# A two-layer hybrid encoder on one core: three changes to the order of TensorE's work

## The chip, the cores and the metric

The program runs on one core of a Trainium2 chip. The metric is the device time of one execution in microseconds, the median of several runs; lower is better. Nothing is computed on the host but the repacking of the weights into chunks.

## The reference

The input is one sequence of 512 tokens with 1024 channels in float32. Each of the two layers is

```
hn = rmsnorm(x); proj = hn @ w_in
(aq, ak, av, bx, by, cq, ck, cv, dq, dk, dv, gl) = split(proj)
ya = dense attention with q/k norm and 2-D rotary      # mixer A, 8 heads on 2 key heads
yb = bidirectional linear recurrence with gates        # mixer B
yc = windowed attention with a sink logit              # mixer C
yd = three dilated window attentions, combined by their softmax denominators   # mixer D
gates = sigmoid(gl + gate_bias)                        # one per branch and channel
merged = sum over branches of gates * (y @ w_proj)
x = x + merged @ w_out
x = x + square(relu(rmsnorm(x) @ w_mlp1)) @ w_mlp2
```

and a last rmsnorm follows. In mixer D three groups of four heads are each normalised by themselves, and the output of a head is the sum of its three group outputs, weighted by a softmax over the groups' log denominators. Those weights are known only when all three groups are done.

## The kernel before

**Weights.** All weights come as chunks of 128x1024 float32 (512 KB) in the order of use. SP loads a chunk into one of three buffers (`raw`, L102), ScalarE (ACT) casts it to the short float32 format (`whi`, L118), and VectorE (DVE) takes the rest, raw minus high (`wlo`, L127). Three pairs of `whi` and `wlo` exist. A load into a `raw` buffer has to wait until cast and difference of the chunk three places earlier have read that buffer. Activations are split in the same way (`xh`, `xl`), and every product of 128 by 128 by 512 is three TensorE matmuls: high by high, high by low, low by high (`mm3`, L173 to L182).

**Which work goes beside which.** The heads of the attentions wait on DVE and ACT for their softmax, so their steps are mixed with steps of plain projections, here called fill. A fill step is a quarter of a gate chunk or half of a short projection: 6 matmuls. `merge` (L1100) mixes two generators a and b: it takes a step of a, then steps of b in the ratio nb to na. `MG` and `E1`, `E2`, `E3`, `FN` (L41, L43) are its tables: na, nb and the number of fill steps that go ahead of the even mixing.

**Attention A.** The loads of its keys and queries (`K`, `Q`) are issued, then the values of A and C are computed (`values_ac`, L527), then `merge` starts. The first step of a is the first head's first score (L796); three fill steps of branch B's gates follow.

**Attention C** is mixed with the values of D (`values_d`, L668): three groups, each with two weight chunks (u = 0, 1) for the contraction's first and second half, and four blocks of 128 tokens; each block is one `mm3` with 24 matmuls of 256 columns, cut into two steps.

**End of mixer D** (`attn_d_end`, L1041). It loads the denominators `W` of the three groups back from DRAM, lets `E1` yields pass, computes the weights on DVE and ACT (L1053 to L1065), transposes them on TensorE (`ps_misc`, L1069), copies the result (`wr`) and stores it to DRAM (`wd`), and then loads it eight times spread over 64 partitions (`wb`, `d_weight`, L1094): that is all three groups of the first half of the heads (hp = 0) and the first group of the second half. After `E2` yields it multiplies and adds the groups of the first half (L1086 to L1089) and splits the sum into `yD`, lets `E3` yields pass, and does the same with the second half; only there the last four `wb` loads are issued. The fill beside it is branch D's own: four gate chunks of 16 steps, and then the projection of `yD`, which is the first thing that needs both halves. The chunk of that projection is called PR below, the gate chunks GL0 to GL3, and the next ones GL4 and on.

All loads and stores named here stand on one queue, SP's, which issues in program order.

Of the kernel before, what the change touches and what calls it, by code (L numbers as in the profile page):

```python
# [37 lines left out]
    "h4 v5 n2 e1 l4 q8 s0 t3 o6 p7",  # L38
)]

MG = ((35, 48, 3), (41, 71, 2), (18, 47, 12))  # L41

E1, E2, E3, FN = (1, 5, 2, 15)  # L43

WU, P0, P1 = (16, 2, 2)

# [29 lines left out]
class Body:  # L76
# [96 lines left out]
    def mm3(self, ps, st, mv, n, step=0):  # L173
        mm = self.nc.tensor.matmul
        for k in range(n):
            (sh, sl), (mh, ml) = st(k), mv(k)
            mm(ps, sh, mh, start=(k == 0), stop=False)  # L177
            mm(ps, sh, ml, start=False, stop=False)  # L178
            mm(ps, sl, mh, start=False, stop=(k == n - 1))  # L179
            if step and k % step == step - 1 and k < n - 1:  # L180
                yield
        self.lows()  # L182

    def several(self, keys, mv, cuts):
# [483 lines left out]
    def values_d(self):  # L668

        nc = self.nc  # L670
        last = []
        for g in range(3):
            hls = self.take2("VD", g)
            for c in range(4):
                ps = self.ps("mm")
                yield from self.paced(last, self.mm3(
                    ps[:, 0:256],
                    lambda k: (self.xh[:, k, c * 128:(c + 1) * 128], self.xl[:, k, c * 128:(c + 1) * 128]),
                    lambda k: tuple(t[:, (k % 4) * 256:(k % 4 + 1) * 256] for t in hls[k // 4]), KD, 4))
                last.append(lambda ps=ps, g=g, c=c: self.value_d(ps, g, c))  # L680
                yield
        while last:
            last.pop()()
# [413 lines left out]
            r = 4 * g + 2 * hp + a  # L1097
            self.nc.sync.dma_start(out=t[64 * a:64 * (a + 1)], in_=wd[r:r + 1, :].to_broadcast([64, S]))

    def merge(self, a, b, na, nb, first=0):  # L1100

        e = 0
        live = [True, True]

        def step(i):
            if live[i] and next((a, b)[i], StopIteration) is StopIteration:
                live[i] = False

        step(0)
        for _ in range(first):  # L1110
            step(1)
        while any(live):
            step(0)
            e += nb - first
            while e >= na or not live[0]:
                step(1)
                e -= na
                if not any(live):
                    break


    def layer(self, l):
# [16 lines left out]
        with tc.tile_pool(name=f"aA{l}", bufs=1, reuse_waits="tile") as self.ap:  # L1139
            attn = self.attn_gqa(l, 0, yA)  # L1140
            next(attn)
            self.values_ac()
            self.merge(attn, self.fill(l, 1, self.yB), *MG[0])
        yC = self.y0p.tile([128, 2, 4, S], F32R, tag="y", name="yC")
        with tc.tile_pool(name=f"aC{l}", bufs=1, reuse_waits="tile") as self.ap:
            self.merge(self.attn_gqa(l, 2, yC), chain(self.values_d(), self.fill(l, 0, yA)), *MG[1])
        yD = y1p.tile([128, 2, 4, S], F32R, tag="y", name="yD")
        fill = self.fill(l, 3, yD)
        with tc.tile_pool(name=f"aD{l}", bufs=1, reuse_waits="tile") as self.ap:
            self.merge(self.attn_d(l, yD), self.fill(l, 2, yC), *MG[2])  # L1150
            self.merge(self.attn_d_end(yD), (next(fill) for _ in range(FN)), E1 + E2 + 1 + 2 * E3, FN)
# [330 lines left out]
```

## Time and profile before

| | |
|---|---|
| median of 3 runs | 2031.62 us (2030.08 to 2032.27) |
| profiled execution | 2030.6 us |
| its span, first to last instruction | 2028.8 us |
| TensorE (PE) busy | 2008.3 us, 99% |
| VectorE (DVE) busy | 1270.8 us, 63% |
| ScalarE (ACT) busy | 974.1 us, 48% |
| share of PE in the chain that ended last | 89% |
| mean granted TensorE clock | 0.996 of full speed |
| DMA, mean over the span | 112 GB/s |

TensorE is the engine to look at: it is busy nearly all the time, so the other engines matter only where TensorE waits for them. Matmul records overlap: a 512-column matmul lasts 0.39 us in its record, and the next one starts 0.228 us after it. So the distance between starts is what a matmul costs.

### The profile page before, as it was taken

How to read it: one execution, taken by the hardware profiler on the slowest of the kernel's cores; microseconds unless marked ns; L12 is line 12 of the kernel's file. 1: busy time of each engine (PE TensorE's matmuls, PEld its weight loads, DVE VectorE, ACT ScalarE, POOL GpSimd, SP SyncE). 2: the span in 40 equal slices, each digit the busy share in tenths (PEclk: the TensorE clock that was granted, in tenths of full speed). 3: DMA queues.
4: the chain of work that ended last, by engine and by line, in shares of the span. 5: the costliest groups of instructions: out<-in, count | busy, mean ns of one | idle time of the engine just before them, and what ended most of it. 6: DMA issues, size and time to landing. Idle time of an engine off the chain costs nothing.

```text
span 2028.8 us, 25698 instructions
## 1 busy us (share of the span) xinstructions
PE 2008.3 (99%) x9752; PEld 1665.0 (82%) x9752; DVE 1270.8 (63%) x2274; ACT 974.1 (48%) x1701; POOL 0.2 (0%) x4
## 2 busy tenths in 40 slices
PE   9999999999999999999999999999999999999998
PEld 7888789887778888888878888898877888888887
DVE  6889775764466544444658897758644665444445
ACT  4357786854534332322323668868445334322322
POOL 0000000000000000000000000000000000000000
PEclk9999999999999999999999999999999999999998
DMA  5454425332134233223335552152421522323231
GB/s 191 136 158 142 130 67 146 116 125 84 53 114 138 94 102 94 96 94 104 123 105 166 156 166 94 62 160 91 135 73 48 173 94 94 104 94 97 94 100 63
DMA packets 87439, 227.03 MB, mean 112 GB/s; under 512 B 15098, under 2 KB 21370, under 8 KB 87316
## 3 DMA queue, kind: packets, MB, share of 16 engines
q1 hardware_dynamic: 84436, 221.20, 34.5%
q10 hardware_dynamic: 2880, 4.20, 0.6%
q8 instruction: 77, 1.26, 0.3%
q14 instruction: 46, 0.38, 0.1%
HBM read 201.08 MB, written 24.27 MB: 111 GB/s over the span
## 4 chain that ended last, share of the span: by engine, by line
PE 89%; DVE 6%; ACT 2%; issue 1%; DMA 1%; SPq 0%; DVEq 0%; ACTq 0%
PE ps_mm L177 13%; PE ps_mm L178 13%; PE ps_mm L179 13%; PE ps_s L177 6%; PE ps_s L178 6%; PE ps_s L179 6%; PE ps_t L177 6%; PE ps_t L179 6%; PE ps_t L178 6%; PE ps_o L856 2%; PE ps_t L835 2%; PE ps_s L796 1%; PE ps_s L797 1%; DVE tt L338 1%; DVE wlo L127 1%
## 5 line engine op out<-in xcount | busy, mean ns | idle before, releaser
L118 ACT CAST whi<-raw 128x1024 fp32r<-128x1024 f32 (+1 forms) x318 | 329.0, 1041 | 334.9 <-PE ps_mm L178 105.6
L127 DVE TENSOR_TENSOR wlo<-raw,whi 128x1024 fp32r<-128x1024 f32 (+1 forms) x318 | 385.0, 1215 | 98.6 <-ACT whi L118 95.6
L177 PE MATMUL ps_mm<-xh,whi 128*128 128x512 f32 x720 | 289.0, 401 | 0.0
L179 PE MATMUL ps_mm<-xh,wlo 128*128 128x512 f32 x720 | 282.6, 392 | 0.0
L178 PE MATMUL ps_mm<-xl,whi 128*128 128x512 f32 x720 | 282.5, 392 | 0.0
L177 PEld LDWEIGHTS ps_mm<-xh,whi 128*128 128x128 f32 x720 | 136.1, 189 | 32.4 <-issue 4.1
L179 PEld LDWEIGHTS ps_mm<-xh,wlo 128*128 128x128 f32 x720 | 135.9, 189 | 29.8
L178 PEld LDWEIGHTS ps_mm<-xl,whi 128*128 128x128 f32 x720 | 136.2, 189 | 26.7
L177 PE MATMUL ps_t<-xh,whi 128*128 128x512 f32 x368 | 143.7, 390 | 0.0
L178 PE MATMUL ps_t<-xl,whi 128*128 128x512 f32 x368 | 143.3, 389 | 0.0
L179 PE MATMUL ps_t<-xh,wlo 128*128 128x512 f32 x368 | 143.2, 389 | 0.0
L177 PE MATMUL ps_s<-xh,whi 128*128 128x512 f32 x352 | 138.6, 394 | 0.0
L179 PE MATMUL ps_s<-xh,wlo 128*128 128x512 f32 x352 | 137.1, 390 | 0.0
L178 PE MATMUL ps_s<-xl,whi 128*128 128x512 f32 x352 | 137.0, 389 | 0.0
L845 DVE TENSOR_TENSOR PT<-ps_t,PT 128x512 fp32r<-128x512 f32 (+2 forms) x128 | 75.1, 587 | 63.9 <-ACT PT L842 54.7
L829 ACT ACTIVATE P<-P,al 128x512 f32<-128x512 f32 (+2 forms) x128 | 82.6, 645 | 17.0 <-DVE al L828 15.7
L719 DVE TENSOR_TENSOR gt<-ps_mm,rb 128x512 f32<-128x512 f32 x54 | 37.2, 688 | 78.3 <-PE ps_mm L179 77.9
L842 ACT CAST PT<-ps_t 128x512 fp32r<-128x512 f32 (+2 forms) x128 | 63.8, 500 | 46.6 <-PE ps_o L856 43.1
L177 PEld LDWEIGHTS ps_t<-xh,whi 128*128 128x128 f32 x368 | 69.1, 188 | 17.3 <-issue 3.0
L179 PEld LDWEIGHTS ps_t<-xh,wlo 128*128 128x128 f32 x368 | 69.1, 188 | 14.3
L178 PEld LDWEIGHTS ps_t<-xl,whi 128*128 128x128 f32 x368 | 69.1, 188 | 14.2
L177 PEld LDWEIGHTS ps_s<-xh,whi 128*128 128x128 f32 x352 | 66.1, 188 | 14.9 <-issue 1.4
(423 smaller groups left out, 4218.2 us busy)
## 6 DMA issues: line engine op xcount, KB each, us to landing
raw<-in_w_dram SPq DMA_DIRECT2D x314, 512.0 KB, 3.5
qsA<-stk SPq DMA_DIRECT2D x32, 128.0 KB, 2.3
qsC<-stk SPq DMA_DIRECT2D x32, 128.0 KB, 2.3
K<-ks SPq DMA_DIRECT2D x16, 256.0 KB, 6.0
Q<-qsA SPq DMA_DIRECT2D x16, 256.0 KB, 3.8
Q<-qsC SPq DMA_DIRECT2D x16, 256.0 KB, 7.0
qD<-stkf SPq DMA_DIRECT2D x24, 128.0 KB, 2.2
kD<-stkf SPq DMA_DIRECT2D x24, 128.0 KB, 2.2
```

The costliest lines, as they stand in the source:

```text
L118: self.nc.scalar.copy(hi[:, s], self.raws[i][:, s])
L127: self.nc.vector.tensor_tensor(out=lo[:, s], in0=raw[:, s], in1=hi[:, s].bitcast(F32), op=ALU.subtract)
L177: mm(ps, sh, mh, start=(k == 0), stop=False)
L178: mm(ps, sh, ml, start=False, stop=False)
L179: mm(ps, sl, mh, start=False, stop=(k == n - 1))
L338: nv.tensor_tensor(out=o, in0=a, in1=b, op=ALU.mult)
L719: nv.tensor_tensor(out=g, in0=ps, in1=self.rb, op=ALU.mult)
L829: ns.activation(out=P[:, 0:n], in_=P[:, 0:n], func=AF.Copy, scale=ls)
L835: nc.tensor.transpose(pt[:, b * 128:(b + 1) * 128], P[:, b * 128:(b + 1) * 128], self.ident)
L842: ns.copy(st["dst"][0], st["src"])
L845: nv.tensor_tensor(out=st["dst"][1], in0=st["src"], in1=st["dst"][0].bitcast(F32), op=ALU.subtract)
L856: nc.tensor.matmul(o, a, b, start=(n_ == 0), stop=(n_ == len(mm) - 1))
```

## The change

Three places change. First, ahead of attention A's first score four fill steps are issued (before: none), and one more behind it; `MG[0]` has a fourth number for that, and `merge` an argument. Second, `E1` goes from 1 to 3 and `FN` from 15 to 17: two more fill steps stand between the loads of `W` and the transposition of the weights, and the fill beside the end of mixer D is two steps longer. Third, the values of D use `mm3s` in place of `mm3`: the same 24 matmuls a block, but the eight that read the low part of the weights come last; the cut into two steps stays at 12 matmuls.

```diff
-MG = ((35, 48, 3), (41, 71, 2), (18, 47, 12))
-E1, E2, E3, FN = (1, 5, 2, 15)
+MG = ((35, 48, 5, 4), (41, 71, 2), (18, 47, 12))
+E1, E2, E3, FN = (3, 5, 2, 17)
...
+    def mm3s(self, ps, st, mv, n, step=0):
+
+        mm = self.nc.tensor.matmul
+        for k in range(n):
+            (sh, sl), mh = st(k), mv(k)[0]
+            mm(ps, sh, mh, start=(k == 0), stop=False)
+            mm(ps, sl, mh, start=False, stop=False)
+            if step and 4 * k == 3 * n - 4:
+                yield
+        for k in range(n):
+            mm(ps, st(k)[0], mv(k)[1], start=False, stop=(k == n - 1))
+        self.lows()
...
-                yield from self.paced(last, self.mm3(
+                yield from self.paced(last, self.mm3s(
...
-    def merge(self, a, b, na, nb, first=0):
+    def merge(self, a, b, na, nb, first=0, before=0):
...
-        step(0)
-        for _ in range(first):
-            step(1)
+        for i in range(first + 1):
+            if i == before:
+                step(0)
+            if i < first:
+                step(1)
```

**TensorE around the first score of attention A in the first layer.** `ps_t` belongs to the last block of values, `ps_mm` to a gate chunk. Before:

```order
L179 MATMUL ps_t_1947<-whi_1758,xl_84 128x256
L796 MATMUL ps_s_1976<-K_1852,Q_1855 128x512 [waits DMAHW2_49,DMAHW3_49,DMAHW1_49,DVE_49]
L797 MATMUL ps_s_1976<-K_1852,Q_1855 128x512
L177 MATMUL ps_mm_1985<-xh_83,whi_1792 128x512 [waits DVE_49,Activation_49]
L178 MATMUL ps_mm_1985<-xl_84,whi_1792 128x512
```

Now, where all 24 matmuls of the first gate chunk (weights `whi_1792`) stand ahead, and the first step of the second chunk (`whi_1974`, `wlo_1975`) comes right behind the score:

```order
L177 MATMUL ps_mm_1980<-xh_83,whi_1792 128x512
L178 MATMUL ps_mm_1980<-xl_84,whi_1792 128x512
L179 MATMUL ps_mm_1980<-xh_83,wlo_1793 128x512
L809 MATMUL ps_s_2010<-K_1852,Q_1855 128x512 [waits DMAHW3_49,DMAHW2_49,DMAHW1_49]
L810 MATMUL ps_s_2010<-K_1852,Q_1855 128x512
L177 MATMUL ps_mm_2020<-xh_83,whi_1974 128x512 [waits DVE_49,Activation_49]
L178 MATMUL ps_mm_2020<-xl_84,whi_1974 128x512
L179 MATMUL ps_mm_2020<-xh_83,wlo_1975 128x512 [waits DVE_49]
```

The score has moved behind a whole gate chunk, and the second gate chunk's weights are now wanted directly after it.

**SP's queue at the end of mixer D in the first layer.** `wb` are the spread weights, `raw` the weight chunks. Before:

```order
L1098 DMA wb_5631<-wd_4736 64x512
L102 DMA raw_5657<-in_w_dram 128x1024 [waits DMAHW2_49,DVE_49]
L102 DMA raw_5698<-in_w_dram 128x1024 [waits DMAHW3_49,DVE_49]
L1098 DMA wb_5716<-wd_4736 64x512 [waits DMAHW4_49,DVE_49]
L1098 DMA wb_5716<-wd_4736 64x512 [waits DMAHW5_49]
L1098 DMA wb_5720<-wd_4736 64x512 [waits DMAHW6_49,DVE_49]
L1098 DMA wb_5720<-wd_4736 64x512 [waits DMAHW7_49]
L102 DMA raw_5745<-in_w_dram 128x1024 [waits DMAHW0_49,DVE_49,Activation_49]
```

Now:

```order
L1111 DMA wb_5643<-wd_4736 64x512
L102 DMA raw_5657<-in_w_dram 128x1024 [waits DMAHW2_49,DVE_49,Activation_49]
L102 DMA raw_5691<-in_w_dram 128x1024 [waits DMAHW3_49,DVE_49]
L102 DMA raw_5732<-in_w_dram 128x1024 [waits DMAHW4_49,DVE_49,Activation_49]
L1111 DMA wb_5744<-wd_4736 64x512 [waits DMAHW5_49]
L1111 DMA wb_5744<-wd_4736 64x512 [waits DMAHW6_49]
L1111 DMA wb_5748<-wd_4736 64x512 [waits DMAHW7_49]
L1111 DMA wb_5748<-wd_4736 64x512 [waits DMAHW0_49]
```

The third `raw` load, which reuses the buffer of the PR chunk and so waits for that chunk's cast and difference, now stands ahead of the last four `wb` loads; before, it stood behind them.

**DVE at the same place.** The `og` rows multiply and add the groups of the second half of the heads; the `wlo` row without another wait is that of the PR chunk. Before:

```order
L719 TENSOR_TENSOR gt_5687<-ps_s_5659,rb_86 128x512 [waits PE_49]
L1086 TENSOR_TENSOR og_5301<-og_5301,wb_5631 128x512 [waits DMAHW1_49,DMAHW0_49]
L1086 TENSOR_TENSOR og_5474<-og_5474,wb_5716 128x512 [waits DMAHW5_49,DMAHW4_49]
L1086 TENSOR_TENSOR og_5575<-og_5575,wb_5720 128x512 [waits DMAHW7_49,DMAHW6_49]
L1088 TENSOR_TENSOR og_5301<-og_5301,og_5474 128x512 [waits DVE_49]
L1089 TENSOR_TENSOR og_5301<-og_5301,og_5575 128x512 [waits DVE_49]
L159 TENSOR_TENSOR yD_4728<-og_5301,yD_4728 128x512 [waits Activation_49]
L127 TENSOR_TENSOR wlo_5696<-raw_5605,whi_5695 128x1024
```

Now:

```order
L159 TENSOR_TENSOR yD_4728<-og_5118,yD_4728 128x512 [waits Activation_49]
L127 TENSOR_TENSOR wlo_5689<-raw_5585,whi_5688 128x1024 [waits DMAHW0_49]
L732 TENSOR_TENSOR gt_5728<-ps_t_5693,rb_86 128x512 [waits PE_49]
L1099 TENSOR_TENSOR og_5301<-og_5301,wb_5643 128x512 [waits DMAHW1_49,DMAHW0_49]
L1099 TENSOR_TENSOR og_5474<-og_5474,wb_5744 128x512 [waits DMAHW6_49,DMAHW5_49]
L1099 TENSOR_TENSOR og_5575<-og_5575,wb_5748 128x512 [waits DMAHW7_49,DMAHW0_49]
L1101 TENSOR_TENSOR og_5301<-og_5301,og_5474 128x512 [waits DVE_49]
L1102 TENSOR_TENSOR og_5301<-og_5301,og_5575 128x512 [waits DVE_49]
L159 TENSOR_TENSOR yD_4728<-og_5301,yD_4728 128x512 [waits Activation_49]
```

The PR chunk's difference has moved from behind the second half to between the first half (`og_5118`) and the second; the gates of GL1 (`gt_5687`) and GL2 (`gt_5728`) have moved up as well, each ahead of a half.

## Rows read from the trace of the kernel before

**Rows 1.** Busy time on the page (us, share of the span, instructions).
```profile
PE 2008.3 (99%) x9752; PEld 1665.0 (82%) x9752; DVE 1270.8 (63%) x2274; ACT 974.1 (48%) x1701; POOL 0.2 (0%) x4
```
**Rows 2.** Waits of PE: line <- releaser: us in total, times, longest.
```profile
PE ps_misc L1069 <- DVE w L1065: 2.0, 2, 1.0
...
PE ps_mm L178 <- DVE wlo L127: 1.3, 2, 0.6
```
**Rows 3.** Timeline of PE: first score of attention A, both layers (start, us).
```profile
210.68 0.47 PE L796 MATMUL ps_s<-K,Q 128*128 128x512 f32 x1 [2.50 <-DVE btq L652]
...
1211.35 0.47 PE L796 MATMUL ps_s<-K,Q 128*128 128x512 f32 x1 [2.25 <-DMA Q<-qsA]
```
**Rows 4.** Chain that ended last, second layer, ahead of that score (start, us, what).
```profile
1207.14 4.07 DMA Q<-qsA
```
**Rows 5.** Timeline of PE: nine gate matmuls behind it, second layer.
```profile
1212.81 0.59 PE L178 MATMUL ps_mm<-xl,whi 128*128 128x512 f32 x1
...
1216.46 0.39 PE L178 MATMUL ps_mm<-xl,whi 128*128 128x512 f32 x1
```
**Rows 6.** Timelines of ACT and DVE around the first score, first layer.
```profile
212.62 2.01 ACT L118 CAST whi<-raw 128x1024 fp32r<-128x1024 f32 x2
214.65 1.28 ACT L808 ACT_TABLE_LOAD   x1
...
213.56 0.68 DVE L806 TENSOR_REDUCE am<-ps_s 128x1 f32<-128x512 f32 x1
...
214.36 2.36 DVE L127 TENSOR_TENSOR wlo<-raw,whi 128x1024 fp32r<-128x1024 f32 x2
```
**Rows 7.** Timelines of ACT, DVE and PE in the values of D, first layer.
```profile
334.12 1.98 ACT L118 CAST whi<-raw 128x1024 fp32r<-128x1024 f32 x2
...
335.18 2.36 DVE L127 TENSOR_TENSOR wlo<-raw,whi 128x1024 fp32r<-128x1024 f32 x2 [1.55 <-ACT whi L118]
...
336.46 0.39 PE L178 MATMUL ps_mm<-wlo,xh 128*128 128x256 f32 x1 [0.64 <-DVE wlo L127]
```
**Rows 8.** Timeline of PE at the end of D, first layer.
```profile
564.38 1.04 PE L1069 MATMUL ps_misc<-cs,w 128*12 128x128 f32 x8 [0.98 <-DVE w L1065]
565.35 0.50 PE L177 MATMUL ps_mm<-xh,whi 128*128 128x512 f32 x1
```
**Rows 9.** Timeline of SP's queue at the end of D, first layer.
```profile
567.75 5.18 SPq L1098 DMA_DIRECT2D wb<-wd  x8
573.02 1.01 SPq L102 DMA_DIRECT2D raw<-in_w_dram  x2
574.12 2.37 SPq L1098 DMA_DIRECT2D wb<-wd  x4
585.80 18.22 SPq L102 DMA_DIRECT2D raw<-in_w_dram  x5
```
**Rows 10.** Timelines of DVE and PE behind that, first layer.
```profile
569.81 0.69 DVE L719 TENSOR_TENSOR gt<-ps_mm,rb 128x512 f32<-128x512 f32 x1 [2.54 <-PE ps_mm L179]
...
574.07 0.69 DVE L1086 TENSOR_TENSOR og<-og,wb 128x512 f32<-128x512 f32 x1 [0.62 <-DMA wb<-wd]
...
576.78 0.69 DVE L159 TENSOR_TENSOR yD<-og,yD 128x512 fp32r<-128x512 f32 x1 [0.69 <-ACT yD L158]
...
580.60 1.29 DVE L1086 TENSOR_TENSOR og<-og,wb 128x512 f32<-128x512 f32 x2 [1.92 <-DMA wb<-wd]
...
583.91 0.69 DVE L159 TENSOR_TENSOR yD<-og,yD 128x512 fp32r<-128x512 f32 x1 [0.69 <-ACT yD L158]
584.51 1.22 DVE L127 TENSOR_TENSOR wlo<-raw,whi 128x1024 fp32r<-128x1024 f32 x1
...
585.93 0.39 PE L177 MATMUL ps_s<-yD,whi 128*128 128x512 f32 x1
```
**Rows 11.** DMA issues from 567.7, then from 574.1: KB each, us to landing.
```profile
wb<-wd SPq DMA_DIRECT2D x1, 128.0 KB, 2.9
...
wb<-wd SPq DMA_DIRECT2D x1, 128.0 KB, 5.9
```

## The prediction

> **What bounds the kernel now.** I read the busy times first [rows 1]: TensorE is busy 99% of the span, so only its own time or its waits can be gained. The list of PE's waits comes next, then the timeline of each place that the change touches, because the cause that a list names can be another than the one that ends last. Three places count. The first score of attention A waits 2.50 us in the first layer and 2.25 in the second [rows 3]. In the second layer the load of the query ends at 1207.14 + 4.07 = 1211.21, and the score starts 0.14 later [rows 4]; the first layer has the same order of loads, so I take the load as the cause there too, whatever DVE name stands beside it. The transposition of D's weights waits 2.0 us in both layers together, and the low parts of a chunk in the values of D 1.3 [rows 2]. That is 8.0 us of waits. There is one more loss: behind the wait of the second layer nine matmuls take 1216.46 - 1212.81 = 3.65 us instead of 9 x 0.23 [rows 5]. That is half clock, 1.2 in place of 2.4 GHz, and costs 1.6 us. Behind the slightly longer wait of the first layer it does not occur.
>
> The sum is made against the profiled execution, 2030.6 us, which is 1.0 below the median of the three runs, 2031.62. About 0.2%, 4 us, is what a measurement of this kernel can tell from no change. A fill step is 6 matmuls; between 565.35 and 585.93 stand 15 of them [rows 8, 10], so one costs 1.37 us.
>
> **First part: fill ahead of attention A's first score.** No work is added. The first gate chunk, 4 steps or 5.5 us, starts at about 208.1, where PE now begins to wait, so the score comes at 213.6 in the first layer. The query is there by 210.7, so the wait goes: -2.50 and -2.25. But two things come in its place. First, the second gate chunk is wanted right behind the score, its low part with the third matmul, at 214.1 + 2 x 0.23 = 214.5. Its cast ends at about 213.65, the middle of the pair that starts at 212.62, and its difference takes 1.2 us, half of the pair of 2.36 [rows 6]. In the order of now it stands where DVE starts the score's maximum at 213.56, so it runs from 213.7 to 214.9: a new wait of 0.4. Second, the score's maximum now stands behind both differences and a gate (214.9 + 1.2 + 0.6 = 216.7), its scale is ready at 217.4, and on ACT a third cast, the table load of 1.28 and the gate's tanh stand ahead of the exponential, which ends at about 218.3. The third score needs that one's PSUM buffer and is due at 217.65: 0.65 more. So 1.1 us in each layer comes back. Net -1.4 in the first layer and -1.15 in the second. With the wait goes its half clock in the second layer: -1.6. Bounds: if nothing comes back, -4.75 and -1.6; if everything does, 0, and the half clock with it.
>
> **Second part: low parts last in the values of D.** 12 matmuls stand ahead of the cut as before. The wait of 0.64 [rows 7] is for the low part of the second half's chunk, ready at 335.18 + 1.2 = 336.4. Now the cast is wanted four matmuls earlier, at about 335.05, and ends at 335.1 or a little later; the low part is wanted twelve matmuls after that, at 336.6. So 0.1 replaces 0.64, in both layers: -1.1. Bounds 0 and -1.3. The matmuls are the same in number and shape.
>
> **Third part: the end of mixer D.** The two added steps cover the wait for the weights: without it PE would transpose at 563.4; with two steps more it does so at 563.4 + 2.74 = 566.15. The weights are ready at 564.38 [rows 8], plus 1.0 for a cast that now stands ahead of their exponentials on ACT; still 0.8 in hand. So -0.98 in each layer.
>
> What follows, however, starts 1.76 us later than before against a PE that is 0.98 earlier, and there is the queue. Step by step, on the first layer's clock:
> - The copy, the store and the eight first `wb` loads shift with the transposition: the third pair of weights, taken at 574.07 now [rows 10], comes at about 575.8.
> - GL1 ends on PE at 566.15 + 0.97 + 5 x 1.37 = 574.0. Its gate is now ahead of the first half on DVE: 574.2 to 574.8. The three products start at 574.8, 575.45 and 576.1, none late. From the third one to the first half's low part are 576.78 - 574.07 = 2.7 [rows 10], so that starts at 578.8.
> - Then comes the PR chunk's difference, which used to stand behind the second half: 579.45 to 580.7.
> - Only now may SP issue the third `raw` load. That this load waits for just this difference is seen before: the difference ends at 584.51 + 1.22 = 585.73, and SP goes on at 585.80 [rows 9, 10]. Behind it stand the last four `wb` loads, issued at 574.12 before. They come at 581.2 to 583.6, the last one starting at about 583.0.
> - A `wb` load lands 2.9 us after its issue when alone and 5.9 behind two weight chunks [rows 11]. Here it is one chunk with a start of over 2 us, so I take 3.2, nearest to the first: 586.2. From the last product to the end of the low part of the second half were 583.91 + 0.64 - 581.2 = 3.35 us, so `yD` is whole at 589.55, and its high part 0.7 before.
> - PE wants the high part with the fourth matmul of the projection, at 585.93 - 0.98 + 0.7 = 585.65. It waits 3.2 us there and 0.45 at the next matmul: **3.65 us of new wait in each layer**, 3.35 if the load lands in 2.9, 6.35 if in 5.9.
>
> The Trainium skill (DMA: Bandwidth & Descriptors, Queues, rings and completion order) says that each DMA engine takes one queue's descriptors in ring order. The 5.9 us behind two chunks agree. By that rule alone, without a start for the chunk, the landing would be between the two rows, at 4.4, and the sum 2.4 us more.
>
> Nothing hides the wait: in-order PE has only the projection's own matmuls behind it. The new waits are longer than those of attention A, of which one in two was followed by half clock; so I take one episode of 1.6 us for the two layers; bounds 0 and 3.2.
>
> The Trainium skill (TensorE: Matmul & The Clock Gate, Part 1) holds that "the default state is throttled, and activity releases the throttle". Of the two waits in the trace one agrees and one does not; by the rule both new waits would bring half clock, and the sum would be 1.6 higher.
>
> **Sum.** 2030.6 - 1.4 - 1.15 - 1.6 - 1.1 - 1.95 + 7.3 + 1.6 = **2032.3 us**, within 0.2% of the median before. The gains of 7.2 are eaten by the wait that one moved load makes.
>
> **Rivals.**
> 1. *The second half's weights come in time after all* (chance 0.15): the queue is not held up, say because the difference or the load gets through earlier than my chain has it. Then neither 7.3 nor its 1.6 is paid: 2023.4, faster. Against it: the load's wait for the difference is seen in both orders, and from 580.7 on even the least landing leaves PE waiting 3.35. For it: the chain has ten links, each read from another order.
> 2. *The last weights land late* (0.20), slower. Place: the four `wb` loads behind the chunk. Price: each us of landing costs 1 us in each layer. It decides from a landing of 4.9 on, where the sum passes 2035.7; with 5.9 the waits are 6.35, the sum 2037.7, and with half clock behind both 2039.3. For it: 5.4 to 5.9 is what these very loads took behind two chunks. Against: there is one chunk now, and DMA is idle before it.
> 3. *Attention A gives everything back* (0.05): the softmax chain, now behind two differences and a gate, costs PE the whole 2.55 that I counted. 2034.9. Against: before, DVE and ACT had caught up within a few steps.
>
> That the change does nothing is no rival, since all three places are in the order of the engines.
>
> **How the numbers follow.** The forecast has 0.60. Its own range is 2027.5 (landing 2.9, no half clock, nothing given back at the first score) to 2036. The range of 2027.0 to 2038.5 adds most of rivals 2 and 3 and leaves out rival 1 and the end of rival 2, under 0.2 together. Faster by over 0.2% (below 2027.6): rival 1 and the lowest edge of the forecast, 0.18. Slower by over 0.2% (above 2035.7): rival 2 and upper edges, 0.25. Same: 0.57.
>
> **What would show it.** Right: no wait at the first score, but about 0.4 at the third matmul of the second gate chunk; the wait of the values of D below 0.2; no wait at the weights' transposition; and PE waiting 3 to 4 us for `yD` in the projection's fourth matmul, behind four `wb` loads that SP issues some 7 us later than before, just after the PR chunk's difference. Wrong: if PE does not wait there, the third part is a plain gain and the kernel faster; if the waits are 5 us or more, or the clock halves in more places than one, it is slower.

## The result, and the profile after

The changed kernel takes **2047.08 us**, median of 4 runs (2046.79 to 2047.54), against 2031.12 (2030.08 to 2032.27) for the kernel before on the same chip: a ratio of 1.0084, 95% interval 1.0071 to 1.0098. It is slower by 16 us, and above the range. The profiled execution takes 2047.2 us, its span is 2045.4.

The line of busy times on the page of the changed kernel answers to [rows 1]: PE has 6.8 us more, though the number of its matmuls is the same, and that is the first hint that some ran slowly.

```profile
PE 2015.1 (99%) x9752; PEld 1667.0 (81%) x9752; DVE 1268.6 (62%) x2274; ACT 975.5 (48%) x1701; POOL 0.2 (0%) x4
```

The list of PE's waits answers to [rows 2] (total us, times, longest). The waits at the first score, for the weights of D and for low parts in the values of D are gone from it. Two new lines, of 7.9 and 7.2 us, come to nearly twice what went (2.5, 2.2, 2.0 and 1.3).

```profile
PE ps_s L177 <- ACT yD L158: 7.9, 2, 4.0
PE ps_s L809 <- ACT P L821: 7.2, 2, 3.7
...
PE ps_o L869 <- DVE PT L858: 1.7, 4, 0.5
PE ps_mm L179 <- DVE wlo L127: 0.9, 2, 0.4
```

**Where the time went.** I compare starts of the same PE instructions in both traces: the last matmul of attention A's and C's values, the first score of attention C, its last score, and the first matmul of the output projection. Each stretch between two of them, less the same stretch before:

| stretch | first layer | second layer | predicted |
|---|---|---|---|
| attention A (last value to C's first score) | +3.57 | +4.85 | -1.4, -2.75 with half clock |
| values of D (C's scores) | -0.57 | -0.66 | -0.55 each |
| D and its end | +6.29 | +5.15 | +2.67 each, and 1.6 for both |
| all the rest together | -2.0 | | 0 |

The last row is what is left of the 16.6 us between the two spans; the change touches nothing there. The next views show the two large ones.

**Attention A**, PE's timeline in the first layer, answers to [rows 3]. The first score waits no longer, the second gate chunk's low part costs 0.43, and the third score waits 3.67:

```profile
212.86 0.39 PE L809 MATMUL ps_s<-K,Q 128*128 128x512 f32 x1
...
214.37 0.50 PE L179 MATMUL ps_mm<-xh,wlo 128*128 128x512 f32 x1 [0.43 <-DVE wlo L127]
...
221.06 0.50 PE L809 MATMUL ps_s<-K,Q 128*128 128x512 f32 x1 [3.67 <-ACT P L821]
```

ACT's timeline at that time answers to [rows 6]. The third cast doesn't start behind the two others but stands 3.17 us for its load; the table load, the gate and the exponential (L821) stand behind it in order.

```profile
211.99 2.01 ACT L118 CAST whi<-raw 128x1024 fp32r<-128x1024 f32 x2
217.17 1.04 ACT L118 CAST whi<-raw 128x1024 fp32r<-128x1024 f32 x1 [3.17 <-DMA raw<-in_w_dram]
218.23 1.28 ACT L733 ACT_TABLE_LOAD   x1
219.53 0.72 ACT L733 ACTIVATE gt<-gt,d_hb 128x512 f32<-128x512 f32 x1
220.15 0.76 ACT L821 ACTIVATE P<-ps_s,an,rqs 128x512 f32<-128x512 f32 x1
```

SP issued that load only behind seven loads of keys and queries (the start and length of the issue):

```profile
208.60 0.54 SPq L102 DMA_DIRECT2D raw<-in_w_dram  x1
```

**End of D.** SP's queue and DVE in the first layer answer to [rows 9] and [rows 10]. The third `raw` load of the three is issued by 583.26, behind the end of the PR chunk's difference at 582.88; the four `wb` loads follow; the second half's last two products start at 588.78, and `yD` begins its low part at 592.09.

```profile
576.99 6.27 SPq L102 DMA_DIRECT2D raw<-in_w_dram  x3
583.32 2.37 SPq L1111 DMA_DIRECT2D wb<-wd  x4
```

```profile
581.66 1.22 DVE L127 TENSOR_TENSOR wlo<-raw,whi 128x1024 fp32r<-128x1024 f32 x1
...
588.78 1.29 DVE L1099 TENSOR_TENSOR og<-og,wb 128x512 f32<-128x512 f32 x2 [4.71 <-DMA wb<-wd]
...
592.09 0.69 DVE L159 TENSOR_TENSOR yD<-og,yD 128x512 fp32r<-128x512 f32 x1 [0.68 <-ACT yD L158]
```

On PE the projection's fourth matmul waits 4.05, and behind it 14 steps from one matmul to the next take 6.28 us in place of 14 x 0.228 = 3.19:

```profile
592.11 0.79 PE L177 MATMUL ps_s<-yD,whi 128*128 128x512 f32 x1 [4.05 <-ACT yD L158]
...
598.39 0.39 PE L179 MATMUL ps_mm<-yD,wlo 128*128 128x512 f32 x1
```

That is half clock, as the windows of PE show (length, busy time, granted clock, DMA share, GB/s). It stands behind the waits for `yD` in both layers, and in attention A of the second layer. Behind the wait of 3.67 in attention A of the first layer (first line) the clock stays full:

```profile
220.00:230.00 10.00, 8.94 (x45) 1.00 0.25 79
...
590.00:600.00 10.00, 7.89 (x21) 0.66 0.30 105
...
1230.00:1240.00 10.00, 9.48 (x34) 0.68 0.24 79
...
1600.00:1610.00 10.00, 5.95 (x18) 0.83 0.29 90
```

### The profile page after: what moved, and what is told of

Read it like the earlier page. It is cut to its first block, busy times and chain, and to the rows that moved or that the text cites. A ratio compares the mean times of both kernels' runs of the same rounds, so it can differ in the third digit from the quotient of the medians.

```text
span 2045.4 us, 25692 instructions
## 1 busy us (share of the span) xinstructions
PE 2015.1 (99%) x9752; PEld 1667.0 (81%) x9752; DVE 1268.6 (62%) x2274; ACT 975.5 (48%) x1701; POOL 0.2 (0%) x4
## 3 DMA queue, kind: packets, MB, share of 16 engines
q8 instruction: 77, 1.26, 0.3%
## 4 chain that ended last, share of the span: by engine, by line
PE 94%; DVE 2%; ACT 1%; DMA 1%; issue 1%; SPq 1%; DVEq 0%; ACTq 0%
PE ps_mm L177 12%; PE ps_mm L179 12%; PE ps_mm L178 12%; PE ps_t L177 7%; PE ps_t L179 7%; PE ps_t L178 7%; PE ps_s L177 6%; PE ps_s L178 6%; PE ps_s L179 6%; PE ps_o L869 2%; PE ps_t L848 2%; PE ps_s L809 1%; PE ps_mm L189 1%; PE ps_s L810 1%; PE ps_mm L190 1%; PE ps_mm L194 1%
```

## The experiments

Times are told as ratios to the kernel before on the same chip (median 2029.3 to 2030.4 there, 2031.1 for the changed kernel), with their 95% interval. A difference of 1 us is hard to see in them, since single runs of every kernel differ by some us. So the stretches of the profiled executions stand beside, worked out as in the table above:

| kernel | ratio (interval) | A, layers 1, 2 | values of D | D and its end |
|---|---|---|---|---|
| changed kernel | 1.0084 (1.0071 to 1.0098) | +3.57, +4.85 | -0.57, -0.66 | +6.29, +5.15 |
| values_only | 0.9991 (0.9982 to 0.9999) | +1.35, -0.11 | -0.64, -0.65 | +0.81, -0.05 |
| score_only | 1.0044 (1.0028 to 1.0061) | +6.20, +4.66 | +0.11, +0.01 | +0.09, -0.01 |
| d_only | 1.0046 (1.0033 to 1.0060) | -0.03, -1.29 | +0.01, -0.01 | +6.53, +5.65 |
| score_hold | 1.0047 (1.0033 to 1.0060) | +0.81, -0.59 | -0.64, -0.65 | +5.81, +5.45 |
| wb_early | 1.0055 (1.0037 to 1.0074) | +6.20, +2.19 | -0.58, -0.64 | +0.27, +3.50 |
| warm | 1.0062 (1.0046 to 1.0079) | +5.30, +4.17 | -0.52, -0.65 | +4.13, +3.30 |
| best | 1.0000 (0.9990 to 1.0009) | +0.65, -0.68 | -0.65, -0.65 | +1.46, +1.00 |
| best_two | 0.9987 (0.9978 to 0.9996) | -0.02, -1.27 | -0.61, -0.65 | +2.99, -0.72 |
| two_values | 0.9989 (0.9980 to 0.9997) | +0.04, -1.27 | -0.65, -0.67 | -0.01, +0.74 |
| two_e24l | 0.9994 (0.9985 to 1.0003) | +0.02, -1.33 | -0.65, -0.66 | +0.69, -0.04 |
| two_e24 | 0.9981 (0.9972 to 0.9989) | +0.02, -1.27 | -0.64, -0.67 | +0.74, -0.43 |
| two_nolow | 0.9986 (0.9977 to 0.9995) | +0.01, -1.26 | -0.64, -0.66 | +0.14, -0.05 |
| two_noscan | 0.9972 (0.9963 to 0.9982) | -1.75, -2.79 | -0.64, -0.65 | -0.03, -0.01 |

In attention A's second layer the kernel before has 1.6 us of half clock [rows 5], so -1.3 there is about what half clock alone gives. The last two kernels leave out a part of the computation.

### The three parts alone

```diff
# values_only: mm3s, with
 MG = ((35, 48, 3, 0), ...)   E1, E2, E3, FN = (1, 5, 2, 15)
# score_only: mm3, with
 MG = ((35, 48, 5, 4), ...)   E1, E2, E3, FN = (1, 5, 2, 15)
# d_only: mm3, with
 MG = ((35, 48, 3, 0), ...)   E1, E2, E3, FN = (3, 5, 2, 17)
```

> Only the low parts last in the values of D; the two other places as before. Theory 1 (the three parts add up, each lost or won where its waits stand): in the changed kernel PE came out of the values of D 0.6 us (first layer) and 0.7 us (second) earlier against before than it went in, so 1.3 us less here: 2029.7 us against 2031.1, no wait for a low part over 0.2 us. Theory 2 (the gain there was only a side effect of attention A having run 3 us later, which gave DVE time for the differences): the wait of 0.64 us stays in both layers and the time is that of before within 0.3 us.

> Only the fill steps ahead of attention A's first score; mm3 in the values of D and E1, FN as before. Theory 1 (parts add up): the third score waits 3.5 to 3.7 us for the exponential in each layer, two values matmuls wait 0.3 and 0.5 us for DVE's low part of the probabilities, half clock in the second layer only; 3.4 us lost in the first layer and 4.4 in the second, 2038.9 us. Theory 2 (the long wait comes from the changed shape of the whole, and alone this part does what I predicted): wait of 0.65 us, 2027 us.

> Only E1 = 3 and FN = 17; attention A and the values of D as before. Theory 1 (parts add up): PE waits 3.8 to 4.1 us for yD in the fourth matmul of its projection in each layer, with half clock behind both, 6.3 and 5.2 us lost: 2042.6 us. Theory 2 (half clock behind these waits is chance, one time in two): the same waits, but one of the layers without half clock, 2039.5 to 2040.5 us.

Measured: each part does alone what it does in the whole. The low parts last give 0.65 in each layer, with no wait left there. The score's part loses 6.2 and 4.7, with half clock in both layers this time. The D part loses 6.5 and 5.7; its waits, longest 4.9, were both followed by half clock:

```profile
PE ps_s L177 <- ACT yD L158: 8.2, 2, 4.9
```

Theory 1 holds in all three, and the second theory of d_only falls. The time of d_only, 2039.5, is 3 us under the first theory's 2042.6 because two stretches that this part doesn't touch were shorter than in the kernel before: attention A by 1.3 and the rest by 2.0. The clock also explains what doesn't fit: values_only has half clock behind the first score's wait in both layers, d_only in neither (+1.35 and -1.29 in attention A), though both have the order of the kernel before there.

### The cast that waits for its load

```diff
+        self.held = 1 if before else 0
         for i in range(first + 1):
...
+        self.held = 0
```

With `held` at 1 the third gate chunk's cast isn't issued when the second gate chunk is taken, but with the next chunk.

> The changed kernel, but the cast of the third gate chunk isn't put on ACT's queue while the fill steps ahead of the first score are issued; it comes with the next chunk taken, behind the first exponentials. Theory 1 (the third score waits because ACT, in order, holds the exponential behind a cast whose load lands only at 217.2 us): the wait for the exponential falls from 3.6 to about 0.6 us in each layer, no half clock in the second layer, 2047.1 - 6.0 - 2.6 = 2038.5 us. Theory 2 (the exponential is late because its maximum stands behind two differences and a gate on DVE, and a table load and a tanh on ACT): the wait stays above 2.5 us and the time falls by less than 3 us, 2044 us or more.

Measured on ACT, in the first layer: the table load follows the two casts at once, and the exponential starts at 214.91, 8.7 us behind the last value, against 12.9 in the changed kernel.

```profile
212.99 1.28 ACT L733 ACT_TABLE_LOAD   x1
214.28 0.72 ACT L733 ACTIVATE gt<-gt,d_hb 128x512 f32<-128x512 f32 x1
214.91 0.76 ACT L821 ACTIVATE P<-ps_s,an,rqs 128x512 f32<-128x512 f32 x1
```

The third score waits no more at all, and the half clock behind it is gone. Of the 3.57 and 4.85 lost, 2.8 and 5.4 come back; the ratio falls from 1.0084 to 1.0047, 7.5 us. So theory 1 holds: the misplaced cast was the loss. But attention A still isn't faster than before in the first layer. Two casts now come together, and PE waits 1.0 us in each layer for the transposed probabilities instead; the two waits of 0.25 in this line were there before:

```profile
PE ps_t L848 <- DVE PT L858: 2.5, 4, 1.0
```

### The wb loads ahead of the third chunk

```diff
             nv.tensor_tensor(out=o0, in0=o0, in1=OG[2, hp], op=ALU.add)
+            if hp == 0:
+                for g in range(1, 3):
+                    self.d_weight(wb, wd, g, 1)
```

> The changed kernel, but the last four wb loads are issued right behind the first half's products, so that on SP's queue they stand ahead of the third weight chunk instead of behind it; nothing else moves. Theory 1 (the wait for yD comes from that one place in SP's queue): no wait at the yD projection over 0.5 us, no half clock behind it, and the end of D gives 1.0 us in each layer instead of costing 6.3 and 5.2: 2047.1 - 7.4 - 6.2 = 2033.5 us. Theory 2 (the loads are late in any case, since they now start behind two chunks and the chain of products starts later): PE still waits 2 us or more in each layer, 2038 us or more.

Measured: the end of D costs 0.27 in the first layer and 3.50 in the second (half clock of 2.0 among it), in place of 6.29 and 5.15. The place in the queue was the main cause in the first layer and a part of it in the second, so theory 2 has a share: PE still waits 0.56 and 2.15 for the high part of `yD`, where the changed kernel waited 4.05 and 3.83. SP issues the four loads right behind the first half's products, and they still land late, behind two chunks. In the second layer, SP and DVE:

```profile
1583.02 0.97 SPq L102 DMA_DIRECT2D raw<-in_w_dram  x2
1584.08 3.20 SPq L1114 DMA_DIRECT2D wb<-wd  x4
```

```profile
1592.89 1.30 DVE L1099 TENSOR_TENSOR og<-og,wb 128x512 f32<-128x512 f32 x2 [2.81 <-DMA wb<-wd]
```

Their issue ends at 1587.28, and the products that need them start 5.6 us later; in the changed kernel that distance is 588.78 - 585.69 = 3.1. So with two fill steps more ahead of the transposition this chain has little or nothing in hand, even with the loads early; it varies from one execution to the next, since best_two below, with the same end of D, waits 1.68 in the first layer and not at all in the second. That the ratio is as high as 1.0055 comes from attention A, untouched here, with half clock in its first layer this time.

### Is it the standing still that halves the clock?

```diff
+            if keep and k == 0:
+                d = self.misc()
+                for _ in range(keep):
+                    mm(d, self.xh[:, 0, 0:128], self.xh[:, 0])
```

> The changed kernel with 14 matmuls of 512 columns more, whose result nobody reads, between the third and the fourth matmul of the yD projection, where PE waits 4 us: 3.2 us of work in each layer that should lie wholly inside the wait. Theory 1 (half clock behind the wait comes from PE standing still in it): the wait shrinks to about 0.8 us, the granted clock stays full behind it, and 3.1 us in the first layer and 2.0 in the second come back: 2042 us. Theory 2 (the clock falls there for another reason, such as the transfers or the engines that run at the same time): half clock as before behind both, 2047 us.

Measured in the first layer (PE's timeline, then its windows):

```profile
588.60 3.33 PE L183 MATMUL ps_misc<-xh 128*128 128x512 f32 x14
593.17 0.51 PE L177 MATMUL ps_s<-yD,whi 128*128 128x512 f32 x1 [1.24 <-ACT yD L158]
```

```profile
590.00:596.00 6.00, 4.54 (x19) 1.00 0.00 0
596.00:600.00 4.00, 4.00 (x20) 1.00 0.79 261
```

and in the second layer, where the added work ends at 1601.4:

```profile
1600.00:1604.00 4.00, 3.35 (x14) 1.00 0.00 0
1604.00:1608.00 4.00, 4.00 (x19) 1.00 0.71 237
```

`yD` is as late as before, and PE's empty work lies wholly in the wait. The clock stays at 1.00 in both layers, and 6.29 and 5.15 become 4.13 and 3.30. What is left is the wait itself, 3.2 us of it now filled with work that nobody needs. In the changed kernel, d_only and score_hold all six waits for `yD`, of 3.3 to 4.9 us, had half clock behind them; filled, neither of the two has. Theory 1 holds: behind this wait half clock comes from PE standing still. It isn't so behind every long wait: the 3.67 us in attention A above had full clock behind them.

### Both faults mended, and fewer steps ahead

best is the changed kernel with the early `wb` loads, the hold, and the held cast issued by itself:

```diff
+        k = 0
         while any(live):
             step(0)
+            k += 1
+            if before and k == 3:
+                self.held = 0
+                self.ahead(self.n_take - 1)
```

best_two has `MG[0] = (35, 48, 4, 2)` beside.

> The changed kernel with the early wb loads, and with the cast of the third gate chunk put on ACT's queue behind the third exponential, in a place of its own instead of together with the next chunk's. Theory 1 (both faults are single places in a queue): third score without a wait, no second wait of 1.0 us for the transposed probabilities, two waits of 0.3 and 0.5 us per layer at the values of attention A left; attention A gains 1.0 us in the first layer and 2.2 in the second, values of D 1.3, end of D 2.1: 2031.1 - 6.6 = 2024.5 us. Theory 2 (filling ahead only moves the wait of attention A to later places, as the 1.0 us at the transposed probabilities did): attention A gains nothing, 2027.7 us.

> As the run before, but only two fill steps ahead of the first score (2.74 us, just more than the wait that they replace) and two behind it. Theory 1 (two steps cover the loads of the query, and the softmax chain, 2.7 us earlier, keeps the lead that it has in the kernel before): no wait at the first score over 0.2 us, none for the third score, none at the values; attention A gains 2.4 us in the first layer and 3.7 in the second (half clock among it), with the rest as before: 2021.6 us. Theory 2 (the query lands later than the two steps last, or the waits at the values stay): 2023 to 2025 us.

Measured: best is as fast as the kernel before, best_two faster by 0.13%, and neither reaches what theory 1 gave. No wait at the first three scores is over 0.5 us in them, and yet attention A in the first layer takes as long as before (-0.02 in best_two). The lost time is spread; in best_two it is 0.50 at the third score, and three dips of about 0.6 behind it:

```profile
217.81 0.50 PE L809 MATMUL ps_s<-K,Q 128*128 128x512 f32 x1 [0.50 <-ACT P L821]
```

So theory 2 of best holds for attention A, and I had to ask why. The end of D did not give the 2.1 us that both theories of best had: it cost 1.46 and 1.00, with waits of 1.71 and 1.28 for `yD`. The time of best_two, 2027.5, is above both of its theories; 2.0 of the 2.99 in its first layer are half clock behind the wait of 1.68.

### Without the D part, and with one step of it

two_values is best_two with `E1, E2, E3, FN = (1, 5, 2, 15)` and the `wb` loads where they were. two_e24l has `(2, 4, 2, 15)`. two_e24 has that and the early loads.

> Two fill steps ahead of the first score with the third cast put later, low parts last in the values of D, and the end of D as in the kernel before (E1 = 1, FN = 15, wb loads where they were). Theory 1 (the first score's wait was lead that DVE and ACT needed; without it the same time is lost in small waits, and only the half clock that sometimes follows the long wait is won): attention A costs as much as before within 0.5 us a layer without half clock, values of D give 1.3, so 2030.1 - 1.3 - 1.5 = 2027.3 us. Theory 2 (two steps ahead win the 2.5 us as such): 2023 us.

> As two_values, with one fill step more ahead of the transposition of D's weights and one less behind it (E1 = 2, E2 = 4, FN = 15): SP's and DVE's order behind the transposition is that of the kernel before. Theory 1 (the one step covers the wait of 0.98 us, and the chain to yD, which then starts 0.4 us later, has 2 us or more in hand before PE needs it): no wait at the transposition, none at the projection over 0.3 us; 1.9 us less than two_values, 2025.4 us. Theory 2 (the chain to yD has no slack for even one step): the 0.98 us come back at the projection, 2027 us or more.

> As two_e24l, with the last four wb loads right behind the first half's products, where only one weight chunk stands ahead of them on SP's queue. Theory 1 (each chunk ahead of them on the queue makes them land later): they land 3.5 us or less after the last issue, against 4.9 to 6 us with two chunks ahead, yD is done 1 to 2 us earlier than in two_e24l, and PE doesn't wait; the time is that of two_e24l within 1 us, as there is slack in both. Theory 2 (their landing doesn't depend on the chunks ahead): 5 us or more as with two chunks.

Measured: two_values comes out where theory 1 had it (0.9989, expected 2027.3, median 2027.14). In the first layer the wait before cost 2.66 us with its slow start, and now 0.83, 0.62, 0.57 and 0.65 stand in small places behind it, 2.67: all of it is given back. In two_e24l one step doesn't cover the wait at the transposition; 0.59 of 0.98 are left, because the moved step's cast stands ahead of the weights' exponentials on ACT (the waits of PE, then ACT's timeline):

```profile
PE ps_misc L1082 <- DVE w L1078: 1.2, 2, 0.6
```

```profile
561.61 1.07 ACT L118 CAST whi<-raw 128x1024 fp32r<-128x1024 f32 x1
562.57 0.42 ACT L1070 ACTIVATE W<-W 128x16 f32<-128x16 f32 x3
```

The gain of 0.4 a layer is too small for the times to tell, and in the first layer it is used up by a wait of 0.76 in the projection for the low part of the PR chunk, which two_values has in the second layer (0.47) and not in the first. The median, 2028.1, is on the side of theory 2. two_e24 has the lowest ratio of all that compute the whole, 0.9981, some 3 to 4 us ahead of the kernel before; but its interval overlaps with those of two_values and best_two. Its `wb` loads landed no earlier for having one chunk ahead instead of two, against its theory 1; but another chunk now follows directly behind them. From the end of their issue to the first product that waits are 4.5 us in the first layer, and 4.2 in two_e24l (3.2 and 3.4 in the second):

```profile
573.73 2.37 SPq L1114 DMA_DIRECT2D wb<-wd  x4
```

```profile
580.55 0.69 DVE L1099 TENSOR_TENSOR og<-og,wb 128x512 f32<-128x512 f32 x1 [1.59 <-DMA wb<-wd]
```

### Why attention A gives it all back

The first exponential starts 8.0 us behind the last value in the kernel before, 7.8 in best_two and 7.9 in two_values, whether the score waits or not. So something else sets it. I took away two suspects in turn:

```diff
# two_nolow
-            nc.vector.scalar_tensor_tensor(
-                out=self.VV[:, c, :, 64:128], ...
+            nc.gpsimd.memset(self.VV[:, c, :, 64:128].bitcast(F32), 0.0)
# two_noscan, in the step with branch B's scan
+            if (f, d) == (3, 1):
+                return
```

> As two_values, but the low parts of attention A's and C's values (four subtractions of 0.39 us on DVE right ahead of the first score's maximum) are left out and set to zero on another engine. Theory 1 (what is lost in attention A after filling ahead is DVE's and ACT's backlog at its start): the first maximum comes 1.5 us earlier, the first exponential 0.8 us earlier (its table load ends then), the third score's wait of 0.5 us is gone and of the three dips of 0.6 us behind it in the first layer most; 1.5 to 2 us less between the last value and attention C's first score in the first layer. Theory 2 (those dips come from the order of fill and scores itself, whatever DVE has ahead): the wait of 0.5 goes and the three dips stay; 0.7 us less or under.

> As two_values, but the backward recurrence of branch B's last block of 128 channels (a product of 0.67 and a scan of 1.23 us on DVE, next to last ahead of the cast of yB) is left out. Theory 1 (the first exponential hangs on that recurrence: ACT stands idle for it for 5 us, and the cast of yB, four scalings of the values, a weight cast, its difference on DVE and the maximum all stand behind it in order): the first exponential starts 1.8 us nearer to the last value, about 6.1 us behind it in place of 7.9, the third score's wait and most of the dips behind it go, and attention A takes 1.5 to 2 us less in the first layer and about as much in the second. Theory 2 (the order of fill and scores sets the pace): the exponential still starts 7.5 us or more behind the last value, or it comes earlier and the dips stay; less than 0.5 us.

Without the four subtractions nothing changes (+0.01), and both theories fall: DVE, freed, stands for ACT's cast, and the maximum stands behind that chunk's difference in order.

```profile
215.23 1.23 DVE L127 TENSOR_TENSOR wlo<-raw,whi 128x1024 fp32r<-128x1024 f32 x1 [1.63 <-ACT whi L118]
```

ACT, in turn, had stood for branch B. In two_values, on ACT:

```profile
208.69 0.62 ACT L666 CAST yB<-btq 128x512 fp32r<-128x512 f32 x1 [5.12 <-DVE btq L665]
...
213.81 0.78 ACT L821 ACTIVATE P<-ps_s,an,rqs 128x512 f32<-128x512 f32 x1 [0.79 <-DVE an L820]
```

and in two_noscan, where the last value starts at 206.03 instead of 205.93:

```profile
207.03 0.62 ACT L668 CAST yB<-btq 128x512 fp32r<-128x512 f32 x1 [3.35 <-DVE btq L667]
...
212.15 0.78 ACT L823 ACTIVATE P<-ps_s,an,rqs 128x512 f32<-128x512 f32 x1 [0.79 <-DVE an L822]
```

The exponential comes 6.1 us behind the last value, as expected, the third score waits no more, and attention A takes 1.8 and 1.5 us less than in two_values. This is shown, then: the start of attention A hangs on branch B's last recurrence, over the cast of `yB` and ACT's queue. The wait for the query lay beside that chain and cost nothing by itself but the half clock that sometimes followed it. What the shorter chain would give with the score where it was before, I didn't run.

## Why the prediction was wrong

**The end of D: the mechanism was right, and the half clock was mis-sized.** The chain came as it was worked out: the third `raw` load waits for the PR chunk's difference (issued by 583.26; reckoned 580.7, on the old clock, from which the stretches ahead had moved this place by 2.4), the loads come behind it, and PE waits 4.05 and 3.83 + 0.22 where 3.65 was given. The wait at the transposition is gone, worth 1.07 in each layer. The term that failed is "one episode of 1.6 us for the two layers": both waits were followed by half clock, and it cost 3.1 and 2.0. I took the size and the odds from waits of 2.25 to 2.50 and used them for waits of 4. This is most of the 4.5 us that the end of D adds to the 14.9 between forecast and profile. The prediction's own sign of being wrong, the clock halving in more places than one, is what came. The rule of the Trainium skill that I had set beside the rows (TensorE: Matmul & The Clock Gate, Part 1) would have had half clock behind both waits; the windows of 0.66 and 0.83 agree with it. The wait of 3.67 in attention A, with a clock of 1.00 behind it, does not.

**Attention A: a wait that I priced at 0.65 took 3.67.** The step that failed is the one that put "a third cast, the table load of 1.28 and the gate's tanh" ahead of the exponential and let it end "at about 218.3". I gave the cast its duration and never asked when its data would be there. Its load, issued behind seven others, was read at 217.17, and the exponential ended at 220.9. score_hold shows that this one place made the wait. With it came half clock of about 2.8 us in the second layer, more than the 1.6 of the kernel before that I had booked as a gain, and two waits of 0.3 and 0.5 us in each layer for DVE's part of the probabilities, which I didn't have. The wait of 0.4 at the third matmul was right (0.43 and 0.42). Together 12.6 us.

**The gain in attention A did not exist.** Even with the cast mended, -2.50 was no gain, as two_values and two_noscan show. I took the query's load as what ends last, which is true of the score, and not of the stretch. The third rival, that attention A gives everything back, was nearest to this, and even it did not have the faulty cast; I gave it 0.05.

**The values of D** gave 0.57 and 0.66, with 0.55 forecast. The untouched rest (-2.0) is of the size by which it differs between executions of other kernels here (-3.3 to +1.2).

**The rivals.** The first is refuted: the weights did not come in time. The second has its place right, the four loads behind the chunk, but not its condition: the landing took about 3.7, 588.78 less the last issue at 585.1, and not the 4.9 from which the rival was to decide. The end of D still cost 11.4 us, near the 12.4 that a landing of 5.9 was priced at, through the clock. The lower edge of the forecast's own range does not come out of the terms beside it: 2032.3 less 0.6, 1.6 and 2.2 is 2027.9 and not 2027.5, so the forecast did not reach below 2027.6; the outcome doesn't hang on it.

## What to carry to other kernels

When a step is moved ahead, list what it puts on every in-order queue, and for each of these instructions ask when its data lands, not how long it takes: here a cast that nobody needed for eight fill steps held back a softmax. A wait at one instruction is a gain only as far as the next thing that hangs on another engine moves too; compare that one's distance (here the first exponential) before and after. And price a long wait of PE with its aftermath at half clock, taken from waits of the same length.

## What the runs showed of the hardware

In the traces of the kernel before, the changed one and all runs, between 60 and 1990 us, PE stood still in 26 places for 1.2 to 4.9 us. Behind each I looked at the granted clock. Where it fell to half, the matmuls of the next 10 us took 1.7 to 3.3 us longer than the usual distance between matmuls of their shapes (0.2 to 0.5 where it didn't):

| wait, us | places | half clock behind it | clock 1.00 behind it |
|---|---|---|---|
| 3.29 to 4.93 | 13 | 11 | 2 (3.55 and 3.67) |
| 2.15 to 2.74 | 8 | 5 | 3 |
| 1.24 to 1.71 | 5 | 1 (1.68) | 4 |

The same order can show it in one execution and not in the next, so it can be a part of the scatter of single runs, which was up to 8.5 us in the kernel before on one chip. Which of these waits escape, and why, the runs don't settle. Half clock also came once without a wait: in wb_early, behind 16 matmuls of two columns in the second layer's projections (PE's windows):

```profile
1044.00:1048.00 4.00, 4.00 (x26) 0.98 0.43 131
1048.00:1052.00 4.00, 4.00 (x12) 0.59 0.02 4
```

The same four `wb` loads took 2.0 to 5.7 us from the end of their issue to the product that waited longest for them. It was least where the one chunk issued just ahead of them stood alone and none followed for over 7 us, as in the changed kernel (3.1 and 2.5), d_only, score_hold and warm: 2.0 to 3.4. Two chunks ahead, or one ahead and one directly behind, went with 3.2 to 5.7. Whether the chunk behind slows them was not tried by itself.
